# Opening of a diffusion / mLSTM layer: the first half of the tokens ahead of the second, in written order, and one weight block as a plain product

## The chip, the cores and the metric

The kernel runs on one core of a Trainium2 chip. The metric is device time in microseconds (us), the median of several runs. PE is the matrix engine (PEld its weight loads), DVE the vector engine, ACT the scalar engine, POOL the GpSimd, SP the engine that issues most transfers.

## What is computed

The reference is one layer for 128 context tokens and 512 latent tokens, d = 1024. The change touches only its first third, the first feed-forward half step with its modulated norm:

```
def adaln(cvec, w, b):
    m = jax.nn.silu(cvec) @ w + b
    return m.reshape(cvec.shape[0], N_MOD, D_MODEL)

hh = rmsnorm(x, g[0]) * (1 + m[1]) + m[0]
x = x + 0.5 * m[2] * swiglu(hh, w1, w3, w2)      # (silu(hh @ w1) * (hh @ w3)) @ w2, D_FF = 2816
hh = rmsnorm(x, g[1]) * (1 + m[4]) + m[3]
y, ctx_out = token_mixer(hh, ...)                # differential attention and mLSTM
x = x + m[5] * y
...                                              # second feed-forward half step
```

All is float32.

## The kernel before

**Layout.** The 640 tokens lie along the free axis, in two halves of 320 (`HALF`); the 1024 features are eight rows of tiles with 128 partitions (`KT`). The residual is one tile `x` of 128x8x640. Every float32 product is made of three products of a high and a low part (`mm3`: high x high, high x low, low x high): a weight tile is copied to its high part by ACT, and DVE subtracts to get the low part (`wH`/`wL`, `wB`, `wC`, `ww`); the same is done for the activations (`hm`, in `hs.hh`). The hidden width of 2816 is 11 blocks of 256 (`FB`). PE products of 128x128 by 128x320 are shown as `ps_f`.

**Opening, lines 705 to 821.** `Modulate` (705) computes the squares of all eight rows for both halves (`Stats`, 165: ACT squares, DVE adds), sums them over partitions with a product with ones (`ps_ss`), and forms 1/sqrt with a Newton step (`rstd_of`, 154) on DVE. The weights of block 0 (w1 and w3) are loaded and split in two pieces (`weights`, 719), the low parts by POOL and DVE. For each feature row k, `product` (736) multiplies the conditioning with the modulation weights `w_ada_k` (`ps_a`) and copies the result to `small`; `columns` (753) turns it into columns (`ps_at`), adds the bias and forms shift and scale for both halves, and `norm` (764) applies them. The loop of line 801 takes eight steps; each has 18 `ps_f` products: three of block 0's four units, a unit being a column half f and a token half hf, for w1 and w3. The fourth unit (1, 1) follows (814), 48 products. Then `shifts` (788) adds the shift to x itself, which `operand_sums` (330) needs.

**Blocks 1 to 10.** From block 1 on, each weight (a `Granule`, 232) is used in the seven products of a fast 2x2 scheme: over feature halves and column/token halves, `operand_sums` forms sums S1 to S4 of the activations, and `parts` and `sums` (245, 263) the sums of the weights. `parts` makes `wB` and `wC` and three `raw` steps, `sums` makes `ww` (ACT 128x2048, then DVE). One weight costs 7 x 12 = 84 products; plain it would be 96 (`Whole`, 272, does that for the down projection). `products` (406) works through the list `up_work` (509): w1 and w3 of blocks 1 to 10; of each weight the products A11, S1, S2, A12 and S3 come in turn, and the last two (A22, S4) inside the next weight's.

**Between them.** `modulation` (843) is called twice per weight; from the third weight on it lets DVE make the remaining modulation columns (`columns.tile`, 667: two reductions of 128x1024), from `raw_a` tiles that POOL's queue loads, and from `csil` (825), the conditioning, loaded by SP into a pool that takes the place of `x`.

**What sets the order.** The program is written with a tile framework: it orders the instructions of each engine by its own time estimate, and inserts the waits. Instructions passed to `keep_in_program_order` stay in the order in which they are written; before, these are all PE instructions, the table loads on ACT, and the transfers of SP's queue while `in_order` is set. Each engine works through its queue in order.

Of the kernel before, what the change touches and what calls it, by code (L numbers as in the profile page):

```python
# [31 lines left out]
def tile_trunk(ctx: ExitStack, tc: tile.TileContext, a: dict):  # L32
    nc = tc.nc
    act = nc.scalar.activation
    vec = nc.vector
    pool_e = nc.gpsimd

    def tt(eng, out, in0, in1, op):
        return eng.tensor_tensor(out=out, in0=in0, in1=in1, op=op)  # L39

    def stt(out, in0, scalar, in1, op0, op1):
        return vec.scalar_tensor_tensor(out=out, in0=in0, scalar=scalar, in1=in1, op0=op0, op1=op1)  # L42

    def ts(out, in0, s1, op0, s2=None, op1=None):
        if s2 is None:
            vec.tensor_scalar(out=out, in0=in0, scalar1=s1, scalar2=None, op0=op0)
        else:
            vec.tensor_scalar(out=out, in0=in0, scalar1=s1, scalar2=s2, op0=op0, op1=op1)
# [45 lines left out]
    for hf in range(2):  # L94
        dma(x_all[:, :, hf * HALF : (hf + 1) * HALF], a["x"][:, :, hf * HALF : (hf + 1) * HALF])
    sel = load(cp, [128, 2], a["sel"], name="sel")
    b_ada = load(cp, [128, 72], a["b_ada"], name="b_ada")
    g_norm = load(cp, [128, 3, KT], a["g_norm"], name="g_norm")
# [173 lines left out]
    class Whole(Granule):  # L272


        def split(self, fp=None):
            flat = self.raw.rearrange("p k n -> p (k n)")
            n = 512 * self.nk
            if fp is None:
# [5 lines left out]
            for (c0, c1, h), (_, _, lw) in zip(*t):  # L284
# [10 lines left out]
    class HalfStep:  # L295
# [29 lines left out]
        def gate_plain(self, f, hf, p):  # L325
            s = self.silu_tile(f, hf)
            act(s, p[0], AF.Silu)
            tt(vec, self.SO[:, self.Q[f, hf]], p[1], s, ALU.mult)

        def operand_sums(self, pair):  # L330
# [37 lines left out]
            low(S4, 0)  # L368
            low(S4, 1)
# [145 lines left out]
        def run_whole(self, x, gate, final, between):  # L515


            work = self.up_work()
# [10 lines left out]
            self.products(work, between, down[:2])  # L529
# [163 lines left out]
    with ExitStack() as ph:  # L693
# [11 lines left out]
        class Modulate:  # L705


            def __init__(self):
                self.raw, self.row = {}, {}
                self.rs = []  # L710
                x = [x_all[:, d, :] for d in range(KT)]
                st = [Stats(x, hf, ntmp) for hf in range(2)]
                for hf in range(2):
                    for d in range(KT):
                        st[hf].add(d)
                    self.rs.append(st[hf].rstd(psum))
                self.load(0)

            def weights(self, w1, w3):

                W = [[wp.tile([128, 2048], F32R, tag="w" + t, name="wH") for t in "HL"] for _ in range(2)]
                raws = [rawp.tile([128, 2048], F32, tag="raw", name="raw") for _ in range(2)]
                for k in range(2):
                    cs = slice(1024 * k, 1024 * k + 1024)
                    for raw, src, (h, lo), eng in zip(raws, (w1, w3), W, (pool_e, vec)):
                        dma(raw[:, cs], src[:, 4 * k : 4 * k + 4])
                        act(h[:, cs], raw[:, cs], AF.Copy)
                        tt(eng, lo[:, cs], raw[:, cs], h[:, cs].bitcast(F32), ALU.subtract)
                    self.load(k + 1)
                self.load(3)  # L730
                return W

            def load(self, k):
                self.raw[k] = load(fp, [128, 2048], a["w_ada_k"][k], tag=("s1", "s2", "s4", "SO")[k % 4], name="raw_a")

            def product(self, k):
# [9 lines left out]
                vec.tensor_copy(self.row[k], ps[:, :256])  # L746
                if k + 4 < KT:
                    self.load(k + 4)
                if k + 4 == KT - 1:
                    dma(ident, a["ident"])  # L750
                    in_order[0] = False

            def columns(self, k):
# [7 lines left out]
                for hf in range(2):  # L761
                    self.norm(hf, k)

            def norm(self, hf, d):

                c0 = hf * HALF
                S = hs.hh(d, hf)
                for s0, s1, j in SEGS[hf]:
                    xs = x_all[:, d, s0:s1]
                    h, lo = (t[:, s0 - c0 : s1 - c0] for t in S)  # L770
                    sh = m_of(0)[:, d, j : j + 1]
# [4 lines left out]
            def before(self, k):  # L776
                if k == 0:
                    self.product(0)
                    self.columns(0)
                    self.product(1)  # L780
                    self.columns(1)
                    self.product(2)
                elif k + 1 < KT:
                    self.columns(k + 1)
                    if k + 2 < KT:
                        self.product(k + 2)

            def shifts(self):
                for d in range(KT):
                    for s0, s1, j in ((0, NS, 0), (NS, T, 1)):  # L790
                        xs = x_all[:, d, s0:s1]
                        act(xs, xs, AF.Identity, bias=m_of(0)[:, d, j : j + 1])

        psum.order = [6, 7]
        start = Modulate()
        W = start.weights(a["w1a"][0], a["w3a"][0])
        units = [(0, 0), (1, 0), (0, 1)]
        psum.order = list(range(6))
        ps = {u: [acc_tile(psum) for _ in range(2)] for u in units}
        psum.order = [6, 7]  # L800
        for k in range(KT):
            start.before(k)
            for u in units:
                for i in range(2):
                    hs.plain(ps[u][i], W[i], *u, k)
        vec.tensor_copy(identr, ident)
        hs.begin_gated(0)
        for u in units:
            hs.gate_plain(*u, ps[u])
        for i in range(2):  # L810
            hs.up[i].load()
        psum.order = [6, 7, 0, 1, 2, 3, 4, 5]
        ps = [acc_tile(psum) for _ in range(2)]
        for i in range(2):
            for k in range(KT):
                hs.plain(ps[i], W[i], 1, 1, k)
        hs.gate_plain(1, 1, ps)
        start.shifts()
        hs.operand_sums(lambda r: x_all[:, 2 * r : 2 * r + 2, :])
        x_stack.close()  # L820
        hs.store_g(hs.SO, 0)

        ada = ExitStack()
        ada_p = ada.enter_context(tc.tile_pool(name="ada", bufs=1, side="right", reuse_waits="tile"))
        csil = ada_p.tile([128, 2, D], F32, name="csil")
        dma(csil, a["c_rows"].partition_broadcast(128))
        act(csil, csil, AF.Silu)
        nc.sync.dma_start(out=csil_dram, in_=csil[0:1])
        junk = ada_p.tile([128, D], BF16, name="junk")
# [5 lines left out]
        def load_columns(src):  # L835
            raw = ada_p.tile([128, D], F32, tag="raw", name="raw_a", bufs=2)
            nc.gpsimd.dma_start(out=raw, in_=src)
            return raw, junk

        columns.place(14, csil, load_columns)  # L840
        box = {}

        def modulation(i, at):
            if i < 20:
                if at and 2 <= i < 16:
# [56 lines left out]
        hs.run_whole(resid, half_m[:, 0], to_mixing, modulation)  # L902
# [1101 lines left out]
```

## Time and profile before

| | |
|---|---|
| median of 3 runs | 1868.25 us (1867.74 to 1875.11) |
| span of the profiled execution, first to last instruction | 1872.4 us |
| PE busy | 1812.7 us, 97% of the span |
| DVE busy | 1300.2 us, 69% |
| ACT busy | 849.6 us, 45% |
| PE in the chain of work that ended last | 86% |
| HBM read, written | 234.20 MB, 63.63 MB |

The profile is of one execution. Its span runs from the first to the last instruction; the times of the runs are measured around the whole execution, and which of them is the profiled one isn't marked. The page has the busy time of each engine, the span in 40 slices with the granted clock of PE (a share of full speed), and the costliest groups of instructions; further views of the same trace give the timeline (start, duration, engine, line, operation, output<-input, shape, count; in brackets the idle time ahead and what ended it), windows of time with the busy time of each engine, groups by shape (busy us, mean ns), and the waits.

### The profile page before, as it was taken

To read this page: it belongs to the slowest core of one execution; us is meant where nothing else is said; L and a number is where in the kernel's file an instruction comes from. 1 tells how busy PE (TensorE), PEld (TensorE's weight loads), DVE (VectorE), ACT (ScalarE), POOL (GpSimd) and SP (SyncE) were. 2 spreads that over 40 slices of the span, in tenths; PEclk is the share of its full clock that TensorE was granted. 3 is DMA by queue.
4 is the path that set the end of the run, shared out by engine and by line. 5 is a ranking of instruction groups with operands and counts; after the bars stand their busy time and mean duration, and the time that the engine had idled before them with its cause. 6 is when DMAs were issued, how large, how long until landed. Compare 5 with 4: busy or idle time off the path is not lost.

```text
span 1872.4 us, 30753 instructions
## 1 busy us (share of the span) xinstructions
PE 1812.7 (97%) x12658; PEld 1774.4 (95%) x12658; DVE 1300.2 (69%) x2177; ACT 849.6 (45%) x1455; POOL 35.8 (2%) x57
## 2 busy tenths in 40 slices
PE   5899999999999999999999989999999999999999
PEld 4899999999998999999999979999999899999999
DVE  6888886576786675865755537875456778887585
ACT  5644444112554353453454436565235645554232
POOL 1000001110000000000000000000000000000000
PEclk8899999999999999999999999999999999999999
DMA  8344547964324322322222254566442344457972
GB/s 328 119 142 168 192 169 260 382 213 146 118 81 133 123 74 95 120 77 95 98 79 83 74 178 128 187 208 218 167 134 95 130 140 153 171 177 250 336 275 91
DMA packets 127293, 299.81 MB, mean 160 GB/s; under 512 B 9457, under 2 KB 90609, under 8 KB 114353
## 3 DMA queue, kind: packets, MB, share of 16 engines
q1 hardware_dynamic: 117890, 257.49, 40.0%
q0 software_dynamic: 9264, 40.37, 5.9%
q8 instruction: 99, 1.62, 0.4%
q14 instruction: 40, 0.33, 0.0%
HBM read 234.20 MB, written 63.63 MB: 159 GB/s over the span
## 4 chain that ended last, share of the span: by engine, by line
PE 86%; DVE 7%; DMA 4%; ACT 2%; issue 1%; SPq 0%; DVEq 0%; ACTq 0%
PE ps_f L52 41%; PE ps_p L52 22%; PE ps_t L52 12%; PE ps_o L52 2%; PE sc L52 2%; PE ps_n L52 2%; PE ps_u L52 1%; DMA ada<-csil_dram 1%; PE ps_wT L55 1%; DVE ww L39 1%; PE ps_qkT L55 1%; DMA P<-nm_dram 1%; DMA so<-o_dram 0%; DVE wL L39 0%; DMA raw_a<-in_w_ada_c 0%
## 5 line engine op out<-in xcount | busy, mean ns | idle before, releaser
L52 PE MATMUL ps_f<-S,ww 128*128 128x320 f32 x1992 | 322.9, 311 | 6.7 <-ACT ww L267 4.2
L52 PEld LDWEIGHTS ps_f<-S,ww 128*128 128x128 f32 x1992 | 301.1, 189 | 9.7 <-ACT ww L267 4.5
L52 PE MATMUL ps_p<-hH,wH 128*128 128x320 f32 x864 | 274.0, 317 | 3.1 <-ACT aT L1325 2.5
L52 PE MATMUL ps_p<-hH,wL 128*128 128x320 f32 x864 | 267.3, 309 | 0.0
L52 PE MATMUL ps_p<-hL,wH 128*128 128x320 f32 x864 | 267.2, 309 | 0.0
L52 PE MATMUL ps_f<-hm,ww 128*128 128x320 f32 x1248 | 198.2, 311 | 2.0 <-DVE ww L39 2.0
L52 PEld LDWEIGHTS ps_f<-hm,ww 128*128 128x128 f32 x1248 | 188.2, 190 | 2.3 <-DVE ww L39 2.2
L52 PE MATMUL ps_t<-wH,hH 128*128 128x256 f32 x640 | 185.7, 290 | 1.0 <-DVE x L42 1.0
L52 PE MATMUL ps_t<-wH,hL 128*128 128x256 f32 x640 | 181.8, 284 | 0.0
L52 PE MATMUL ps_t<-wL,hH 128*128 128x256 f32 x640 | 181.5, 284 | 0.0
L52 PEld LDWEIGHTS ps_p<-hH,wH 128*128 128x128 f32 x864 | 162.8, 188 | 4.4 <-ACT aT L1325 2.7
L39 DVE TENSOR_TENSOR ww<-raw,ww 128x2048 fp32r<-128x2048 f32 (+1 forms) x62 | 138.7, 2237 | 37.7 <-ACT ww L267 18.7
L52 PEld LDWEIGHTS ps_p<-hL,wH 128*128 128x128 f32 x864 | 162.8, 188 | 0.5
L52 PEld LDWEIGHTS ps_p<-hH,wL 128*128 128x128 f32 x864 | 162.5, 188 | 0.0
L52 PE MATMUL ps_f<-hm,wB 128*128 128x320 f32 x1008 | 161.5, 309 | 0.0
L52 PEld LDWEIGHTS ps_f<-hm,wB 128*128 128x128 f32 x1008 | 151.3, 188 | 0.0
L39 DVE TENSOR_TENSOR wL<-raw,wH 128x2048 fp32r<-128x2048 f32 x49 | 112.1, 2289 | 38.2 <-ACT wH L123 38.1
L123 ACT ACTIVATE wH<-raw 128x2048 fp32r<-128x2048 f32 x49 | 93.6, 1911 | 89.4 <-PE ps_p L52 85.5
L39 DVE TENSOR_TENSOR raw<-raw 128x1024 f32<-128x1024 f32 x144 | 124.6, 865 | 1.9
L52 PEld LDWEIGHTS ps_t<-wH,hH 128*128 128x128 f32 x640 | 123.1, 192 | 2.0 <-issue 1.2
L52 PEld LDWEIGHTS ps_t<-wH,hL 128*128 128x128 f32 x640 | 123.1, 192 | 0.5 <-DVE hL L42 0.5
L52 PEld LDWEIGHTS ps_t<-wL,hH 128*128 128x128 f32 x640 | 123.3, 193 | 0.2
(295 smaller groups left out, 3206.0 us busy)
## 6 DMA issues: line engine op xcount, KB each, us to landing
g_dram<-g SPq DMA_DIRECT2D x44, 640.0 KB, 5.1
raw_a<-in_w_ada_c SPq DMA_DIRECT2D x24, 512.0 KB, 4.0
raw<-in_w1b SPq DMA_DIRECT2D x11, 1024.0 KB, 4.9
raw<-in_w3b SPq DMA_DIRECT2D x11, 1024.0 KB, 4.8
raw<-in_w1a SPq DMA_DIRECT2D x10, 1024.0 KB, 4.8
raw<-in_w3a SPq DMA_DIRECT2D x10, 1024.0 KB, 6.4
ada<-in_w_ada_c POOLq DMA_DIRECT2D x18, 512.0 KB, 5.3
hm<-g_dram POOLq DMA_DIRECT2D x7, 1280.0 KB, 9.6
```

What stands on the lines that cost most here:

```text
L39: return eng.tensor_tensor(out=out, in0=in0, in1=in1, op=op)
L52: tc.keep_in_program_order(nc.tensor.matmul(*args, **kw))
L55: tc.keep_in_program_order(nc.tensor.transpose(*args, **kw))
L123: act(h, raw, AF.Copy)
```

## The change

The helpers `act`, `tt`, `stt`, `ts` pass their instruction through `placed`, which keeps it in written order while `as_written` is set: through the whole opening, ACT and DVE too follow the order of the text. `Opening` takes the place of `Modulate`. x is loaded in four pieces, half 0 first; SP's queue takes modulation weights, weight pieces (four pairs instead of two) and the rest of x in turn. Squares, sums, 1/sqrt, division and norm are done for half 0 first; the first loop multiplies half 0 only (four units of w1 and w3, 12 products a step), with the squares and sums of half 1 between its steps; a second loop of eight steps then multiplies half 1. Shift and scale are applied to x at once, by ACT (half 0) or DVE (half 1). POOL makes no split any more. w1 of block 1 is split whole (into `gA`, `gB`, `CL`) and multiplied plainly, 96 products; the fast scheme begins with w3 of block 1. The last two steps of the operand sums (the lows of S4) and the start of the late columns (`csil` and its loads) move behind the first weights of the fast scheme. In the built program the PE instructions that follow block 1 are the same, in the same order; DVE and ACT differ in some places elsewhere.

```diff
+    def placed(ins):
+        if as_written[0]:
+            tc.keep_in_program_order(ins)
+        return ins
...
+    def load_x(hf, r):
+        dma(x_all[:, 4 * r : 4 * r + 4, hf * HALF : (hf + 1) * HALF], a["x"][:, 4 * r : 4 * r + 4, hf * HALF : (hf + 1) * HALF])
...
-        def operand_sums(self, pair):
+        def operand_sums(self, pair, hold=False):
...
+            def last():
+                low(S4, 0)
+                low(S4, 1)
+            if hold:
+                return last
...
-            self.products(work, between, down[:2])
+            self.products(work, between, down[:2], prepared=True)
...
-        class Modulate:
+        class Opening:
...
+            def squares(self, hf, r):
...
+                xs = x_all[:, 4 * r : 4 * r + 4, half(hf)]
+                act(p, xs[:, 0:2], AF.Square)
+                tt(vec, q, xs[:, 2:4], xs[:, 2:4], ALU.mult)
+                tt(vec, p, p, q, ALU.add)
...
+            def add_squares(self, hf, r):
+                for i in range(2):
+                    mm(self.ss[hf], ones, self.sq[r][:, i], start=r + i == 0, stop=r + i == 2)
...
+            def divide(self, hf, r):
+                xs = x_all[:, 2 * r : 2 * r + 2, half(hf)]
+                tt(vec, xs, xs, self.rs[hf][:, None, :].to_broadcast([128, 2, HALF]), ALU.mult)
...
             def norm(self, hf, d):
...
-                    stt(xs, xs, scale[:, 0, d, j : j + 1], self.rs[hf][:, s0 - c0 : s1 - c0], ALU.mult, ALU.mult)
-                    act(h, xs, AF.Identity, bias=sh)
-                    stt(lo, xs, sh, h.bitcast(F32), ALU.add, ALU.subtract)
+                    act(h[:, s0 - c0 : s1 - c0], xs, AF.Identity, scale=sc, bias=sh)
+                    if hf:
+                        ts(xs, xs, sc, ALU.mult, sh, ALU.add)
+                    else:
+                        act(xs, xs, AF.Identity, scale=sc, bias=sh)
+                tt(vec, lo, self.x[d][:, half(hf)], h.bitcast(F32), ALU.subtract)
...
+        PIECES = ((0, 2), (2, 4), (4, 6), (6, 8))
+        def step(ps, k, hf, between=None):
+            h, lo = hs.hh(k, hf)
+            for m, (w, v) in enumerate(((0, h), (1, h), (0, lo))):
+                for (f, i), p in ps.items():
+                    col = 256 * k + 128 * f
+                    mm(p, W[i][w][:, col : col + 128], v, start=k == 0 and m == 0, stop=k == KT - 1 and m == 2)
+                if m == 0 and between is not None:
+                    between()
...
+        for r in range(2):
+            start.squares(0, r)
+            start.add_squares(0, r)
+        start.product(0)
+        start.load(4)
+        load_weights(3)
+        start.rstd(0)
+        split_weights(0, "high")
+        start.refine(0)
+        start.columns(0)
+        start.divide(0, 0)
+        start.product(1)
+        split_weights(0, "low")
+        start.norm(0, 0)
+        start.load(5)
...
+        first = acc()
...
         for k in range(KT):
+            def ahead(k=k):
+                if k + 1 < KT:
+                    start.columns(k + 1)
+                if k == 5:
+                    start.refine(1)
+                if k >= 6:
+                    start.divide(1, k - 6)
+                if k % 2 and k < 6:
+                    split_weights((k + 1) // 2, "low")
+                elif k % 2 == 0 and k + 2 < KT:
+                    start.divide(0, (k + 2) // 2)
+                if k + 1 < KT:
+                    start.norm(0, k + 1)
+                if k % 2 == 0 and k < 6:
+                    split_weights(k // 2 + 1, "high")
+            step(first, k, 0, ahead)
+            if k + 2 < KT:
+                start.product(k + 2)
+                if k < 2:
+                    start.load(k + 6)
+            if k in (3, 4):
+                start.add_squares(1, k - 3)
+            if k in (1, 2):
+                start.squares(1, k - 1)
+            if k == 4:
+                start.rstd(1)
+            if k >= 6:
+                start.norm(1, k - 6)
...
+        for k in range(KT):
+            if k + 2 < KT:
+                if k in (1, 3):
+                    start.divide(1, (k + 3) // 2)
+                start.norm(1, k + 2)
+            step(second, k, 1)
+            if k == 5:
+                whole.split(t=[((0, 2048, w1[0]),), ((0, 1792, w1[1]), (1792, 2048, w1[2][:, :256]))])
...
+        for f, hf in ((0, 1), (1, 1), (0, 0), (1, 0)):
+            p = acc_tile(psum)
+            for k in range(KT):
+                mm3(p, whole.w(0, k, f), whole.w(1, k, f), *hs.hh(k, hf), k == 0, k == KT - 1)
+            gate_first(f, hf, p, None)
+        with tc.issue_after(end.ins), tc.issue_after(at_act.ins):
+            last_lows = hs.operand_sums(lambda r: x_all[:, 2 * r : 2 * r + 2, :], True)
...
+        def begin_columns():
+            with tc.issue_after(hs.work[1][0].split_at):
+                last_lows()
+            x_stack.close()
...
+                if (i, at) == (1, 1):
+                    begin_columns()
...
-        hs.run_whole(resid, half_m[:, 0], to_mixing, modulation)
+        hs.run_whole(resid, half_m[:, 0], to_mixing, lambda i, at: modulation(i + 1, at))
```

More of the change, by code (lines that the diff above doesn't have):

```diff
@@ L272, in tile_trunk, with split @@
     class Whole(Granule):
-        def split(self, fp=None):
+        def split(self, fp=None, t=None):
             flat = self.raw.rearrange("p k n -> p (k n)")
             n = 512 * self.nk
-            if fp is None:
+            if t is not None:
+                pass
+            elif fp is None:
                 t = [((0, n, h),) for h in self.two(wp, "w", 2048, None)]
@@ L703, in tile_trunk @@
         hs = HalfStep(1, fp, ntmp, psum, a["w1a"], a["w3a"], a["w2a"], FB)
-        class Modulate:
+        class Opening:
             def __init__(self):
[L709 to L731, printed above, removed]
@@ L745, in product @@
                 self.row[k] = mrow[k % 2]
[L746 to L751, printed above, removed]
+                placed(vec.tensor_copy(self.row[k], ps[:, :256]))
             def columns(self, k):
@@ L776, in before @@
[L776 to L800, printed above, removed]
-        for k in range(KT):
[L802 to L806, printed above, removed]
@@ L807, in tile_trunk @@
-        hs.begin_gated(0)
[L808 to L814, printed above, removed]
-            for k in range(KT):
[L816 to L820, printed above, removed]
@@ L821, in tile_trunk @@
-        hs.store_g(hs.SO, 0)
[L823 to L829, printed above, removed]
+                    xs, sc, sh = self.x[d][:, s0:s1], scale[:, 0, d, j : j + 1], m_of(0)[:, d, j : j + 1]
@@ new lines, in tile_trunk, with load_weights, split_weights @@
+        PIECES = ((0, 2), (2, 4), (4, 6), (6, 8))
+        def load_weights(i):
+            k0, k1 = PIECES[i]
+            for raw, src in zip(raws, (a["w1a"][0], a["w3a"][0])):
+                dma(raw[:, 256 * k0 : 256 * k1], src[:, k0:k1])
+        def split_weights(i, part):
+            cs = slice(256 * PIECES[i][0], 256 * PIECES[i][1])
+            for raw, (h, lo) in zip(raws, W):
+                if part != "low":
+                    act(h[:, cs], raw[:, cs], AF.Copy)
+                if part != "high":
+                    tt(vec, lo[:, cs], raw[:, cs], h[:, cs].bitcast(F32), ALU.subtract)
@@ new lines, in step @@
+        def step(ps, k, hf, between=None):
[6 more added lines that the diff above has]
+                    between()
+        acc = lambda: {(f, i): acc_tile(psum) for f in range(2) for i in range(2)}
@@ new lines, in tile_trunk @@
+        as_written[0] = True
+        start = Opening()
+        start.load(0)
+        for t, n in ((sel, "sel"), (b_ada, "b_ada"), (g_norm, "g_norm")):
+            dma(t, a[n])
+        load_weights(0)
+        start.load(1)
+        start.load(2)
+        load_x(1, 0)
+        load_weights(1)
+        start.load(3)
+        load_x(1, 1)
+        load_weights(2)
+        psum.order = [4, 5, 6]
+        for r in range(2):
+            start.squares(0, r)
+            start.add_squares(0, r)
+        start.product(0)
@@ new lines, in tile_trunk @@
+        dma(ident, a["ident"])
+        in_order[0] = False
+        hs.work = hs.up_work()
+        _, _, gate_first, _ = hs.work.pop(0)
+        whole = Whole(4, hs.up[0].fetch)
+        whole.load()
+        hs.up[1].load()
+        hs.begin_gated(0)
+        psum.order = [4, 5, 6, 7, 0, 1, 2, 3]
+        second = acc()
+        w1 = [fp.tile([128, n], F32R, tag=tag, name="w" + tag, bufs=bufs) for tag, n, bufs in (("gA", 2048, 1), ("gB", 1792, 1), ("CL", 512, 3))]
+        for k in range(KT):
[6 more added lines that the diff above has]
+                whole.split(t=[((0, 2048, w1[0]),), ((0, 1792, w1[1]), (1792, 2048, w1[2][:, :256]))])
+                hs.up[2].load()
+                silu_table()
+                for f in range(2):
+                    hs.gate_plain(f, 0, (first[f, 0], first[f, 1]))
@@ L830, in tile_trunk @@
+        with tc.issue_after(end.ins), tc.issue_after(at_act.ins):
+            hs.work[0][0].parts(fp)
+            hs.work[0][0].sums()
+        hs.store_g(hs.SO, 0)
         columns = Columns(56)
@@ L835, in load_columns @@
         def load_columns(src):
-            raw = ada_p.tile([128, D], F32, tag="raw", name="raw_a", bufs=2)
+            raw = ada_p[0].tile([128, D], F32, tag="raw", name="raw_a", bufs=2)
             nc.gpsimd.dma_start(out=raw, in_=src)
-            return raw, junk
-        columns.place(14, csil, load_columns)
+            return raw, ada_p[1]
+        ada = ExitStack()
+        ada_p = []
+        def begin_columns():
+            with tc.issue_after(hs.work[1][0].split_at):
+                last_lows()
+            x_stack.close()
+            pool = ada.enter_context(tc.tile_pool(name="ada", bufs=1, side="right", reuse_waits="tile"))
+            csil = pool.tile([128, 2, D], F32, name="csil")
+            dma(csil, a["c_rows"].partition_broadcast(128))
+            act(csil, csil, AF.Silu)
+            nc.sync.dma_start(out=csil_dram, in_=csil[0:1])
+            ada_p.extend((pool, pool.tile([128, D], BF16, name="junk")))
+            columns.place(14, csil, load_columns)
         box = {}
```

71 lines of the change are left out of this document (49 added, 22 removed).

## The prediction

> **What bounds the kernel now.** First the page, for where the matrix engine is not busy:
>
> ```profile
> span 1872.4 us, 30753 instructions
> ...
> PE   5899999999999999999999989999999999999999
> ...
> PEclk8899999999999999999999999999999999999999
> ```
>
> One slice is 46.8 us. PE is full from the third slice on; the first two miss some 50% and over 10%, at a reduced clock. The stages in windows (us, PE, PEld, DVE, ACT and POOL busy, granted clock, DMA share, GB/s) say how much is at stake:
>
> ```profile
> 0.00:100.00 100.00, 75.18 (x507) 65.11 (x508) 75.76 (x141) 59.34 (x103) 6.37 (x8) 0.90 0.57 216
> 100.00:380.00 280.00, 277.25 (x1869) 275.40 (x1868) 217.54 (x289) 116.01 (x157) 16.71 (x28) 0.99 0.63 219
> ```
>
> 25 us of the first 100 are idle, 2.75 of the next 280. The timeline of the opening (start, duration) shows which:
>
> ```profile
> 8.01 0.47 ACT L177 ACTIVATE nacc<-x 128x320 f32<-128x320 f32 x1 [4.07 <-DMA x<-in_x]
> ...
> 12.41 1.44 PE L52 MATMUL ps_ss<-nacc,ones 128*128 128x320 f32 x2 [12.41 <-DVE nacc L39]
> ...
> 14.95 0.49 DVE L48 TENSOR_SCALAR rv<-ps_ss 128x320 f32<-128x320 f32 x1
> ...
> 17.73 2.35 POOL L39 TENSOR_TENSOR wH<-raw,wH 128x1024 fp32r<-128x1024 f32 x1 [17.28 <-ACT wH L727]
> 17.78 2.65 DVE L42 SCALAR_TENSOR_TENSOR ry<-rt,ry 128x320 f32<-128x320 f32 x1
> ...
> 22.89 1.07 PE L52 MATMUL ps_a<-raw_a,small 128*32 128x256 f32 x16
> ...
> 30.23 4.83 PE L52 MATMUL ps_f<-hm,wH 128*128 128x320 f32 x18
> ...
> 36.33 2.90 PE L52 MATMUL ps_f<-hm,wH 128*128 128x320 f32 x18
> ...
> 40.51 2.90 PE L52 MATMUL ps_f<-hm,wH 128*128 128x320 f32 x18
> ...
> 84.27 0.90 PE L52 MATMUL ps_f<-S,ww 128*128 128x320 f32 x2 [4.22 <-ACT ww L267]
> ...
> 86.60 3.04 PE L52 MATMUL ps_f<-S,ww 128*128 128x320 f32 x10 [1.42 <-DVE ww L39]
> ...
> 96.11 1.92 PE L52 MATMUL ps_f<-hm,wB 128*128 128x320 f32 x12
> ...
> 108.44 1.92 PE L52 MATMUL ps_f<-hm,wB 128*128 128x320 f32 x12
> ```
>
> Two losses: no product of block 0 starts before 30.23, and PE waits 4.22 + 1.42 us for the split weight sums ww of block 1. From 96.11 (block 2's first weight) to 108.44 (its second) 84 products take 12.33: 0.147 us each, no gap. **Both kernels run the same PE stream from there to the end, so the sum is kept at these two marks.** Each loss has a tail at half clock (us, PE busy, granted clock, DMA share, GB/s):
>
> ```profile
> 22.00:24.00 2.00, 1.61 (x20) 1.00 1.02 422
> 24.00:26.00 2.00, 0.00 (x0) 0.57 1.03 426
> ...
> 34.00:36.00 2.00, 2.00 (x22) 0.87 1.02 422
> ...
> 80.00:82.00 2.00, 0.06 (x1) 1.00 0.94 326
> 82.00:84.00 2.00, 0.00 (x0) 0.58 0.80 194
> ...
> 92.00:94.00 2.00, 2.00 (x14) 0.86 0.03 8
> ```
>
> 0.57 means full clock for 0.28 us of the two, so it fell at 24.3 and rose at 34.5; again at 82.3 and 92.6: both times 10.2 us.
>
> **The change part by part.**
>
> *Start of block 0.* The bytes of the first half still land at 8.0. Its squares become one ACT and two DVE instructions on 128x640 per two pairs of rows; the last pair costs two DVE operations of 0.82 (row x<-x below): 9.7 instead of 12.41. From 12.41 to 14.95 two products with ones take 2.5; so 12.3. Next on PE stands the modulation product 0 (1.07 at full clock), and on DVE its copy (0.42) now stands ahead of rv: 13.8. Then rv 0.49, two ACT steps 0.9, three DVE steps of 0.49, mod and scale 0.3, the division 0.82, the ACT norm 0.65: 18.9. **I take 19.0 against 30.23.** The 2.65 for ry, five times rv's 0.49, began with a POOL split (17.73); that split goes, its work moves to DVE as pieces of 128x512.
>
> ```profile
> 490.42 0.70 PE L52 MATMUL ps_ss<-nacc,ones 128*128 128x320 f32 x2
> ...
> L39 DVE TENSOR_TENSOR x<-x 128x640 f32<-128x640 f32 x8 | 6.4, 818 | 0.0
> ...
> L42 DVE SCALAR_TENSOR_TENSOR x<-x,scale,ry 128x192 f32<-128x192 f32 x8 | 3.3, 411 | 0.0
> ...
> L1838 ACT ACTIVATE hm<-x,mod,scale 128x320 fp32r<-128x320 f32 x8 | 4.5, 648 | 0.0
> ...
> L1838 ACT ACTIVATE hm<-x,mod,scale 128x192 fp32r<-128x192 f32 x8 | 4.3, 535 | 2.5 <-DVE x L39 2.5
> ...
> L354 ACT ACTIVATE S<-x 128x640 fp32r<-128x640 f32 x6 | 4.3, 732 | 0.8 <-issue 0.5 <-DVE x L39 0.3
> ...
> L39 DVE TENSOR_TENSOR ww<-raw,ww 128x2048 fp32r<-128x2048 f32 x6 | 13.7, 2291 | 7.0 <-PE ps_f L52 3.7 <-ACT ww L267 3.3
> ...
> L267 ACT ACTIVATE ww<-raw 128x2048 fp32r<-128x2048 f32 x6 | 11.5, 1912 | 8.5 <-PE ps_f L52 8.4
> ...
> L39 DVE TENSOR_TENSOR wB<-raw,wB 128x1024 fp32r<-128x1024 f32 x6 | 7.3, 1222 | 0.7 <-ACT wB L252 0.7
> ...
> L39 DVE TENSOR_TENSOR wC<-raw,wC 128x512 fp32r<-128x512 f32 x7 | 4.8, 685 | 0.0
> ...
> L39 DVE TENSOR_TENSOR g<-SO,g 128x1280 fp32r<-128x1280 f32 x3 | 4.5, 1485 | 0.0
> ...
> L676 DVE CUSTOM_DVE_ANT_0 junk<-raw_a,csil 128x1024 bf16<-128x1024 f32 x6 | 7.3, 1218 | 0.0
> ```
>
> *First half, eight steps.* Before, 36.33 to 40.51 is 4.18 for 18 products: 2.64, plus 1.54 for the modulation. A step now has 12 products: 1.76 + 1.54 = 3.3, six times; the last two have less modulation (2.3 and 1.8): 23.9. The second half's sums now stand inside: two pairs at about 1.1 (from 490.42, at full clock): 2.2. Half clock for the first step or so: +2 (18 products took 4.83, not 2.9). Written order on DVE: two squares (1.5) stand ahead of mod and scale of row 3; ACT's two norm steps (1.3) and the low (0.5) come after, then the copy that step 3's ps_at needs: PE, with 2.2 of products and 1.0 of modulation to do meanwhile, waits some 0.7. In step 5 the refinement (1.5), two splits (1.4), a low (0.5) and the copy (0.4), 3.7 after the scale, stand ahead of step 6's ps_at; PE has 2.3: 1.4. Sum 30.2, **end at 49.2**. Loads: 13.1 MB of x, modulation and first weights at the 0.42 MB/us of the windows, 1.31 of them landed by 8.0, end near 37; SP's queue is now x, modulation and weight pieces in turn, and its last modulation weight is needed at about 43. Block 1's two weights stand behind it and behind the last split (45), land some 8 later and are needed at 59. Hidden.
>
> *Second half and the plain product.* 96 products each: 14.1 + 14.1, **77.4**. The second half's norm runs ahead under them: per row of tiles ACT 0.54 + under 0.5, DVE at most 0.41 + 0.35 (two pieces, priced as the two-tensor form), a low of 0.49 and half a division, 1.7, against PE's 1.76. Nothing is charged; without that cover, 0.3 a step. The plain form has 96 products where 84 stood: 12 x 0.147 = 1.8, in the sum.
>
> *Block 1's second weight.* Its S1 needs ww. ACT in its queue waits for the silu of the plain product's third unit (end 73.9) before the copy of S2's second half: silu 0.43, copy 0.73, then DVE: three lows and two terms at about 0.74 (818 ns less overlap), ww 2.29: 81.1. PE has done its first product at 79.2: **a wait of 1.9** takes the place of 4.22 + 1.42 and their tail. Four more products: block 2's mark at 88.1 against 96.11, **8.0 ahead**.
>
> *Given back after it.* Next ww: wB 1.14, wC 0.6, g 1.4, raw 1.14 + 0.6 + 0.6, the ACT half 1.91, ww 2.29 = 9.7 after the last ww; PE takes five products, 8.8: **0.9**. The late columns: the load of csil now stands behind the S4 lows, 1.9 after that ww. From there 5.1 to ACT (below), 1.91 of silu, 2.6 for two reductions that stand ahead of the next ww, 2.29: 11.9, while PE has 12.3 - 1.9 = 10.4: **1.5**.
>
> ```profile
> 81.30 0.35 SPq L74 DMA_DIRECT2D csil<-in_c_rows  x1
> ...
> 86.41 1.91 ACT L827 ACTIVATE csil<-csil 128x2048 f32<-128x2048 f32 x1 [2.19 <-DMA csil<-in_c_rows]
> ```
>
> **Sum: 8.0 - 0.9 - 1.5 = 5.6 us gained.** The rest of the program keeps its PE order; some DVE and ACT instructions change places under a full PE: 0, at most 1 either way. The profiled span of 1872.4 becomes 1866.8. That span is 4.15 above the median of 1868.25 (runs from 1867.74 to 1875.11; what lies around the span comes on top and stays), so the gain is taken off the median: **1862.6**.
>
> *Unknown costs.* The half clock in the first step: between 0 (already at full clock) and twice 2. The two waits in the loop: 0 to 4. The three ww waits: 0 each if ACT and DVE run as they do after 96, or up to before's 5.6 for the first; I take the queues as added up, since every instruction in them has a row. Bounds together: 5.6 + 4.3 + 2.1 + 1 = 13 gained, 5.6 - 2 - 1.9 - 3.7 = 2 lost, and 1 for the order elsewhere: 1855 to 1871.
>
> *A rule weighed.* The clock fell at 24.3 although PE had been busy 1.61 of the two us before 24; at 82.3 it fell 2.4 us after PE's last work near 79.9. So something between a stretch with gaps and 2.4 us of idle suffices, and 1.9 us of waiting may. [...]
>
> **The rivals.**
>
> 1. *The waits don't come* (DVE and ACT get ahead): the three ww waits (4.3) and the loop's 2.1 go, gain 11 to 12: 1857. For it: ACT is at 59% in the opening. Against: the queues hold an order that PE's progress gates (silu ahead of copies).
> 2. *The start is early but given back*: the loop runs at DVE's pace. DVE has some 23 us of work in the 30 (copies, splits, divisions, lows and squares at the durations above), in written order, each step waiting for ps_at; 0.7 us more per step for semaphores takes 5.6: 1868. That is also where it ends if the early start is only spent waiting. For it: before, DVE is 76% busy here and the chain of waits runs through it.
> 3. *Half clock again, slower*: the place is the S1 wait, and again the csil wait. If the first grows to before's 4.2 (+2.3), the clock falls and ten microseconds pass at half of it (+5); the same at csil: 14.6 against a gain of 5.6: 9 slower, about 1877. It decides below the 2.4 us of idle after which the clock fell at 82.3, at 1.9 to 2.4. For it: just this happened at 82.3. Against: my waits are 1.9 and less, with a full PE before and after.
>
> **How the numbers follow.** Forecast (gain 3 to 9.3) 0.48; rival 1 0.27; rival 2 (gain under 3, loss under 3) 0.18; rival 3 0.07. Faster or slower by 0.5% is 9.3 us, about what a measurement of this kernel can tell from no change: faster 0.27, same 0.67, slower 0.06. The range takes in the forecast, most of rivals 1 and 2: 1855 to 1871.
>
> **What would show it.** Right: first ps_f product near 19; the last of the first half near 49; the plain product's last near 77; one wait of some 2 us for ww after it; block 2's marks near 88 and 101. Wrong: a loop of 35 us or more, granted clock at 0.5 after 26 or after 80, or a first block 2 mark after 93; on the other side, no wait for ww at all.

## The result, and the profile after

The change made the kernel a little slower. Over 20 runs of each, the changed kernel took 1875.92 us (median, 1870.05 to 1882.19) and the kernel before 1873.76 (1867.74 to 1876.32); the ratio is 1.0018, 95% interval 1.001 to 1.0025. The forecast was 1862.6, 5.6 below a median of three runs, 1868.25; with more runs that median itself stands 5.5 higher.

The page of the changed kernel: span, busy tenths of PE in 40 slices, and granted clock.

```profile
span 1874.8 us, 30757 instructions
...
PE   7999999999999999999999989999999899999999
...
PEclk9999999999999999999999999999999899999999
```

The first slices, which the change is about, are fuller (7 and 9 where 5 and 8 stood). But the slice near 1500 us, which was full before, now shows an 8 in both rows (the slice from 1453 to 1500). The windows (us, PE busy, granted clock, DMA share, GB/s) of after put sizes to it:

```profile
0.00:100.00 100.00, 82.62 (x575) 0.97 0.58 215
100.00:380.00 280.00, 276.74 (x1874) 1.00 0.65 227
380.00:1480.00 1100.00, 1070.55 (x7618) 0.99 0.37 124
1480.00:1510.00 30.00, 25.86 (x159) 0.89 0.52 177
```

and the last of these windows in the kernel before:

```profile
1480.00:1510.00 30.00, 30.00 (x205) 1.00 0.63 229
```

PE gained 7.4 busy us in the first 100, and lost 4.1 in thirty microseconds that lie 1400 us further on, in code that the change doesn't touch: the opening of the second feed-forward half step. The timeline of PE after (start, duration, engine, line, operation, tiles, shape, count, idle time ahead and its releaser), first in the opening:

```profile
18.64 1.08 PE L59 MATMUL ps_f<-hm,wH 128*128 128x320 f32 x4 [2.43 <-ACT hm L43]
...
63.29 0.46 PE L59 MATMUL ps_f<-hm,wgA 128*128 128x320 f32 x2
...
77.37 1.92 PE L59 MATMUL ps_f<-hm,wB 128*128 128x320 f32 x12
79.13 0.46 PE L59 MATMUL ps_f<-S,ww 128*128 128x320 f32 x2
81.23 3.49 PE L59 MATMUL ps_f<-S,ww 128*128 128x320 f32 x22 [1.64 <-DVE ww L46]
84.56 1.92 PE L59 MATMUL ps_f<-hm,wB 128*128 128x320 f32 x12
89.22 2.31 PE L59 MATMUL ps_f<-S,ww 128*128 128x320 f32 x12 [2.75 <-ACT u L43]
91.33 3.22 PE L59 MATMUL ps_f<-hm,wB 128*128 128x320 f32 x12
94.38 1.92 PE L59 MATMUL ps_f<-S,ww 128*128 128x320 f32 x12
```

Up to 85 this is the forecast to 0.4 us: first product at 18.64 (19.0 forecast), plain product from 63.29 to 77.37 (77.4), a wait of 1.64 for ww (1.9). Then comes a wait that the forecast hasn't: 2.75 us for the copy u, and a stretch at half clock behind it (granted 0.50 from 91 to 94; 3.22 us for twelve products that take 1.92 elsewhere). In the second half step the two kernels' PE rows, after:

```profile
1485.15 1.92 PE L59 MATMUL ps_f<-hm,wB 128*128 128x320 f32 x12
1489.46 0.57 PE L59 MATMUL ps_f<-S,ww 128*128 128x320 f32 x2 [2.38 <-ACT ww L43]
1491.79 3.04 PE L59 MATMUL ps_f<-S,ww 128*128 128x320 f32 x10 [1.76 <-DVE ww L46]
1494.62 3.03 PE L59 MATMUL ps_f<-hm,ww 128*128 128x320 f32 x12
1497.48 1.92 PE L59 MATMUL ps_f<-S,ww 128*128 128x320 f32 x12
```

and before:

```profile
1490.00 1.92 PE L52 MATMUL ps_f<-hm,wB 128*128 128x320 f32 x12
1491.76 2.17 PE L52 MATMUL ps_f<-S,ww 128*128 128x320 f32 x12
1493.77 1.92 PE L52 MATMUL ps_f<-hm,ww 128*128 128x320 f32 x12
1495.53 1.92 PE L52 MATMUL ps_f<-S,ww 128*128 128x320 f32 x12
```

Where PE was 4.85 us ahead (1485.15 against 1490.00) it leaves 1.95 late (1497.48 against 1495.53): 6.8 us lost on 36 products, 4.1 by waiting and the rest at half clock (granted 0.50 from 1492 to 1496, where before had 1.00).

Following the same product in both traces gives where the lead stood:

| product | before | after | lead |
|---|---|---|---|
| block 2's first weight, A11 | 99.64 | 91.33 | 8.3 |
| the S1 products behind it | 101.39 | 94.38 | 7.0 |
| first product of the token mixer (ps_t) | 488.19 | 480.37 | 7.8 |
| second half step, second weight, A11 | 1490.00 | 1485.15 | 4.9 |
| 36 products later | 1495.53 | 1497.48 | -1.95 |
| last row of PE | 1866.93 | 1869.15 | -2.2 |

Of the 7.8 at the token mixer, 1.5 is not the change's work. The kernel before lost it near 360, where its clock fell behind a wait of 1.96 (0.70 from 358 to 360, then 0.50; last section): the same product stands at 357.91 and 351.61 ahead of that, 6.3 apart, and at 362.76 and 354.94 behind it, 7.8 apart.

### The profile page after: what moved, and what is told of

Its sections match the earlier page's. It is cut to its first block, busy times and chain, and to the rows that moved or that the text cites. A ratio compares the mean times of both kernels' runs of the same rounds, so it can differ in the third digit from the quotient of the medians.

```text
span 1874.8 us, 30757 instructions
## 1 busy us (share of the span) xinstructions
PE 1816.8 (97%) x12678; PEld 1776.7 (95%) x12678; DVE 1295.3 (69%) x2165; ACT 842.7 (45%) x1435; POOL 31.0 (2%) x55
## 4 chain that ended last, share of the span: by engine, by line
PE 83%; DVE 8%; DMA 5%; ACT 2%; issue 1%; SPq 0%; DVEq 0%; ACTq 0%
PE ps_f L59 39%; PE ps_p L59 20%; PE ps_t L59 12%; PE ps_o L59 2%; PE sc L59 2%; PE ps_n L59 2%; DMA ada<-csil_dram 1%; DVE ww L46 1%; PE ps_wT L62 1%; PE ps_qkT L62 1%; DMA P<-nm_dram 1%; PE ps_u L59 1%; DMA hm<-g_dram 1%; DVE raw_a L697 1%; PE ps_ss L59 1%
## 5 line engine op out<-in xcount | busy, mean ns | idle before, releaser
L59 PE MATMUL ps_f<-S,ww 128*128 128x320 f32 x1956 | 315.9, 311 | 9.5 <-DVE ww L46 4.0
L59 PEld LDWEIGHTS ps_f<-S,ww 128*128 128x128 f32 x1956 | 294.4, 188 | 12.4 <-DVE ww L46 6.7
L43 ACT ACTIVATE ww<-raw 128x2048 fp32r<-128x2048 f32 (+1 forms) x61 | 114.1, 1871 | 157.6 <-PE ps_f L59 97.1
L43 ACT ACTIVATE wH<-raw 128x2048 fp32r<-128x2048 f32 (+1 forms) x57 | 98.2, 1729 | 89.0 <-PE ps_p L59 84.3
```

What stands on the lines that cost most here:

```text
L43: return placed(nc.scalar.activation(*args, **kw))
L59: tc.keep_in_program_order(nc.tensor.matmul(*args, **kw))
```

## The experiments

Two theories stood against each other at either place. **Order:** the instruction that PE waits for is ready to run, but stands behind others in the queue of ACT or DVE, which wait themselves. **Rival:** its data comes when it comes (a load, a chain that doesn't move with PE), so that any lead is eaten there. The queues' orders can be edited without touching anything else: the listing of the built program gives the order on each engine, and edges that order issue only, with no wait for completion, pin it.

```diff
+    def queue(engine, order):
+        ins = [i for i in tc.nc.cur_bb.bb.instructions if str(i.engine) == engine and ...]
+        for p, n in zip(order, order[1:]):
+            tc.add_manual_dep(ins[-n], ins[-p].name, mybir.DependencyInfo(mybir.DependencyClass.NoSync, ...), reason="queue")
```

In all of these but fast_w1 every other instruction on PE, ACT, DVE and POOL keeps its place; with the order of the second half step, two loads of x on SP move too. The first two runs exchange that place between the kernels.

**late_as_before.** The changed kernel with 19 ACT and 27 DVE instructions near 1470 to 1500 in the order of before. The core of it on ACT:

```diff
 u
-wB
-s
-u
-s
-ps_f
+wC
 ww
+wB
+s
+u
+ps_f
+s
```

> The changed kernel, whose ACT and DVE queues stand in the order of the kernel before in one place only: the opening of the second feed-forward half step, near 1470 to 1500 us (19 ACT and 27 DVE instructions). Theory T (the lead is lost there to the order of the two queues): the waits of 2.38 and 1.76 for ww at 1487 to 1492 and the half clock behind them go, 6.8 us less than the changed kernel, 1869 against the 1873.8 of the kernel before, ratio near 0.9975. Rival R (ww comes at 1492 in both kernels because something that does not move with the lead delivers it, so the order is not the cause): the waits stay, 1876, ratio near 1.002.

Measured: 1871.19 (11 runs), ratio to before 0.9993 (0.9984 to 1.0001); the changed kernel stood at 1.0018. The wait for ww is gone, as PE's rows of this run show:

```profile
1486.67 1.92 PE L59 MATMUL ps_f<-hm,wB 128*128 128x320 f32 x12
1488.43 1.92 PE L59 MATMUL ps_f<-S,ww 128*128 128x320 f32 x12
```

ww is there at 1488.4, so nothing holds it until 1492: the rival falls. In the traces the place is worth what was expected: this execution came to it 1.5 us behind that of the changed kernel (A11 of the half step's first fast weight at 1477.87 against 1476.35) and left it 5.5 ahead (1491.95 against 1497.48 for the product behind the 36), 7 us in all. By the medians and by the two ratios the gain is 4.7 us, less than 6.8; where the other runs lose the rest is not shown.

**before_late_as_after.** The same edit the other way round: the kernel before, with the changed kernel's order in that place.

> The kernel before, with the ACT and DVE orders of the changed kernel in the same one place, the opening of the second feed-forward half step. Theory T: the waits of some 4 us and half clock of up to 2.6 us behind them appear, 4 to 7 us more, 1878 to 1881, ratio 1.002 to 1.0037. Rival R: nothing changes, ratio 1.000.

Measured: 1878.52 (6 runs), ratio 1.0040 (1.0028 to 1.0051), 6.3 us more than before's median beside it (1872.25). The two waits appear with the same lengths, to 0.01 us:

```profile
1490.84 0.56 PE L52 MATMUL ps_f<-S,ww 128*128 128x320 f32 x2 [2.38 <-ACT ww L267]
1493.17 3.04 PE L52 MATMUL ps_f<-S,ww 128*128 128x320 f32 x10 [1.77 <-DVE ww L39]
```

So the order alone, without any of the change's own edits, costs what the changed kernel lost there. Why it is slow is on ACT and DVE, in the changed kernel:

```profile
1484.41 0.42 ACT L43 ACTIVATE s<-ps_f 128x320 f32<-128x320 f32 x1
1485.35 0.44 ACT L43 ACTIVATE u<-ps_f 128x320 f32<-128x320 f32 x1 [0.52 <-PE ps_f L59]
1486.35 0.47 ACT L43 ACTIVATE s<-s 128x320 f32<-128x320 f32 x1 [0.56 <-DVE s L46]
1487.17 0.42 ACT L43 ACTIVATE ps_f<-ps_f 128x320 f32<-128x320 f32 x1 [0.35 <-PE ps_f L59]
1487.51 1.90 ACT L43 ACTIVATE ww<-raw 128x2048 fp32r<-128x2048 f32 x1
```

and on DVE:

```profile
1485.82 0.49 DVE L46 TENSOR_TENSOR s<-ps_f,u 128x320 f32<-128x320 f32 x1 [1.39 <-ACT u L43]
1486.23 0.68 DVE L46 TENSOR_TENSOR raw<-raw 128x512 f32<-128x512 f32 x1
```

The ACT half of ww, which PE needs for its next product, stands behind four small instructions, of which the last can only run when PE has ended the product just before the wait (A11, 1485.15 to 1487). So the splitting of ww starts when PE is already idle, and takes 1.90 on ACT and 2.29 on DVE. ACT alone is not the whole of it: ww also needs the last raw step, and DVE made that only at 1486.23 to 1486.91, behind a step s that waited 1.39 for a copy u, which itself waits for PE. By these rows a better order on ACT alone could have started ww at most 0.6 us earlier. In late_as_before, where both queues stand in the order of before, DVE has the raw steps done by 1483.31 and ACT starts ww at 1484.20, 2.5 us ahead of A11. The two queues were only exchanged together; the share of each was not measured.

**u_first.** In the opening of the changed kernel, ACT's queue after the S4 copies was:

```profile
79.67 1.35 ACT L43 ACTIVATE hm<-x 128x640 fp32r<-128x640 f32 x2
86.15 0.63 ACT L43 ACTIVATE wC<-raw 128x512 fp32r<-128x512 f32 x1 [5.13 <-DMA raw<-in_w3a]
86.94 1.91 ACT L43 ACTIVATE ww<-raw 128x2048 fp32r<-128x2048 f32 x1 [0.16 <-DVE raw L46]
88.75 0.42 ACT L43 ACTIVATE u<-ps_f 128x320 f32<-128x320 f32 x1
```

wC belongs to block 2's second weight, whose load was issued at 81.20, when ww of block 1 had freed its buffer (its DVE half ended at 81.17). The copy u, which PE needs for its next product, could have run when S2 ended, at 84.7; it waits until 88.75 behind a load that is needed a whole weight later. In this trace ACT took nothing out of turn: it stood idle for the 5.13 us ahead of wC, and u ran third, behind wC and ww, as the queue has them. The edit:

```diff
 hm hm
+u
 wC
 ww
-u
 wB
```

> The changed kernel with all queues as built but one ACT instruction: the copy u of block 1's second weight stands two places further ahead, before the copy wC of block 2's second weight (which waits 5.13 us for its load) and before ww. Theory: PE's wait of 2.75 at 86.5 to 89.2 goes and so does the half clock of about 1.7 behind it; S1 of block 2's first weight then waits about 1.3 for ww, and some 0.8 comes back at the late columns: 2.5 to 3.3 less than the changed kernel, about 1873, ratio near 1.0000. Rival (the copy only waits for PE's own S2, which ends at 83, or PE then waits as long for ww): less than 1 us less, ratio 1.0015. The place near 1490 is as in the changed kernel by both.

Measured: 1877.92 (7 runs), ratio 1.0033 (1.0021 to 1.0044): no gain. PE's rows of this run:

```profile
86.91 1.92 PE L59 MATMUL ps_f<-hm,wB 128*128 128x320 f32 x12
88.67 1.92 PE L59 MATMUL ps_f<-S,ww 128*128 128x320 f32 x12
...
93.58 1.73 PE L59 MATMUL ps_f<-S,ww 128*128 128x320 f32 x10 [0.94 <-DVE ww L46]
...
108.08 2.37 PE L59 MATMUL ps_f<-S,ww 128*128 128x320 f32 x10 [1.91 <-DVE ww L46]
110.24 2.86 PE L59 MATMUL ps_f<-hm,ww 128*128 128x320 f32 x12
```

The wait for u is gone, as expected; but the next two waits are now 0.94 and 1.91, and behind the second the clock fell, by the rows' lengths (2.37 and 2.86 for rows of 1.73 and 1.92), which cost some 1.6 us more. The 2.75 had been covering the two that the prediction had summed as 0.9 and 1.5. The account comes out at nothing: 2.75 and the half clock of 1.7 behind it went, 0.94, 1.91 and 1.6 came. This execution also ran at half clock until 27.0 at its start and so stood 2.4 us behind the changed kernel's before the edit (A11 of block 1's second weight at 79.73 against 77.37); it is 2.3 behind after these waits (S2 of that next weight at 112.94 against 110.65). That the edit brings nothing by itself is what times and rows both say; that u's wait came from the order is what the rows say.

**both_orders.** u_first and late_as_before together.

> The changed kernel with both edits: the copy u two places further ahead, and the opening of the second feed-forward half step in the order of the kernel before. Theory T: 9 to 10 us less than the changed kernel, about 1866.5, ratio near 0.996. If the losses are not of these orders: 1873 to 1876, ratio 1.000 to 1.002.

Measured: 1869.99 (12 runs), ratio 0.9988 (0.9979 to 0.9997). It beats the kernel before, but by a third of what was expected: the waits of 1.64, 0.94 and 2.00 still stand in the opening.

**queues_by_need.** both_orders, with the ACT and DVE queues of block 1 in the order in which PE needs them: ww ahead of the last S3 low and of the S4 terms, raw steps ahead of g, u ahead of the S4 copies, the third ww ahead of csil's silu and of the column reductions. On DVE, from 75 us:

```diff
 S S
-S x x
 ww
+S
 wB wC
-g
 raw raw raw
+x x
 ww
```

> The kernel of both_orders with the ACT and DVE queues of block 1 put in the order in which PE needs them: ww of block 1's second weight ahead of the S3 low and the S4 terms, the raw steps of the next weight ahead of the S4 terms and of g, the copy u and ww ahead of the S4 copies, and the third ww with its three raw steps ahead of csil's silu and the two column reductions. Theory T (each wait of PE after 78 us stands in these queues, not in a transfer): the waits of 1.64, 0.94 and 2.00 of both_orders go to 0.5 or less each, block 2's first weight begins near 87 and its second near 99, 4 us less than both_orders: about 1866, ratio 0.9965. Rival (the raw loads set the pace, so the waits move to wC or to the next ww): 1870, ratio 0.9988, with a wait for ww of 1 us or more still in the opening.

Measured: 1871.49 (11 runs), ratio 1.0003 (0.9993 to 1.0012). All three waits are gone or small (0.27 at most for ww), as the theory had it; the time is not, since one of 6.86 for the next u has come: on ACT, csil's silu, now ahead of it, waited 6.15 for its load, issued at 93.33 behind two others and landed at 105.7.

**csil_first.** One SP instruction moved, csil's load ahead of those two.

```diff
+csil
 g_dram
 raw
-csil
```

> The kernel of queues_by_need with one SP instruction moved: the load of csil goes out ahead of the second g transfer and of the raw load of block 3's first weight, instead of behind them. Theory (the 6.86 us wait of queues_by_need is the csil load, issued at 93.3 behind these two and landed at 105.7, with csil's silu ahead of the copy u on ACT): csil lands near 97 to 100, the wait for u goes, and what remains is both_orders without its waits of 1.64, 0.94 and 2.00: 3 to 4 us less than both_orders, about 1866.5, ratio 0.9965 to 0.9975. Rival (the wait is not the load's place in the queue but its bytes, 8 loads and stores sharing the same engines): the wait stays at 3 us or more, 1869 to 1871, ratio near 0.999.

Measured: 1869.59 (12 runs), ratio 0.9986 (0.9974 to 0.9997). csil's silu now ran at 101.00 without a wait; but behind it on ACT stood wC of block 3's first weight, waiting for its load until 106.54, and behind that again u: PE waited 4.36. That load, now behind csil and g, had taken from 94.27 to 106.5. By its numbers the rival holds: with this order of ACT, the load that went last was the one waited for in both runs (6.15 us for csil in queues_by_need, 3.64 for this one here).

**copies_first.** So the copies of that weight go behind u, on ACT and DVE:

```diff
 ww csil
-wC
 g
-wB
 s u ps_f
+wC wB
 s s u
```

> The kernel of csil_first with the copies of block 3's first weight (wC, wB on ACT, then on DVE) behind the copy u of block 2's first weight instead of ahead of it: in csil_first wC waited until 106.5 for its load and u stood two places behind, so PE waited 4.36 and the clock fell. Theory (the head of ACT's queue waits for a load that is needed later): that wait goes, no wait for u or ww of 0.5 us or more is left between 78 and 125, and the time is 4 to 6 us less than csil_first's profile, 3 less than both_orders: about 1866.5, ratio 0.9965. Rival (each wait that is taken away comes up at the next weight, since the raw loads land at their own pace): a wait for ww or wB of 2 us or more in the next weight, 1869 to 1871, ratio near 0.9985.

Measured: 1865.31 (7 runs) beside 1872.88 of before (12 runs): ratio 0.9962 (0.9947 to 0.9976), 7.6 us faster than before, and the fastest of all versions. PE's rows:

```profile
79.28 3.72 PE L59 MATMUL ps_f<-S,ww 128*128 128x320 f32 x24
...
86.35 1.92 PE L59 MATMUL ps_f<-hm,wB 128*128 128x320 f32 x12
88.11 0.46 PE L59 MATMUL ps_f<-S,ww 128*128 128x320 f32 x2
88.84 1.73 PE L59 MATMUL ps_f<-S,ww 128*128 128x320 f32 x10 [0.28 <-DVE ww L46]
...
104.05 2.02 PE L59 MATMUL ps_f<-hm,ww 128*128 128x320 f32 x12 [0.54 <-ACT u L43]
```

Block 2's first weight begins at 86.35, 13.3 us ahead of before's 99.64; the waits left are 0.28 to 0.54. Against the changed kernel no product was left out, and in the opening only csil's load was moved among the transfers: the rest of what it gains on that kernel came from what stood ahead of what on ACT and DVE. Not all of the 13.3 reaches the end: 11.4 are left at 104.05 (before: 115.47), and 8.1 at PE's last row (1858.80 against 1866.93). Part of that is the clock, 0.83 from 530 to 540 and from 560 to 570 in this execution, where before's was 1.00 from 530 to 590.

**fast_w1.** The changed kernel without its plain product: block 1's first weight in the fast scheme again.

```diff
-        _, _, gate_first, _ = hs.work.pop(0)
-        whole = Whole(4, hs.up[0].fetch)
-        whole.load()
+        hs.up[0].load()
         hs.up[1].load()
...
-        for f, hf in ((0, 1), (1, 1), (0, 0), (1, 0)):
-            p = acc_tile(psum)
-            for k in range(KT):
-                mm3(p, whole.w(0, k, f), whole.w(1, k, f), *hs.hh(k, hf), k == 0, k == KT - 1)
-            gate_first(f, hf, p, None)
```

> The changed kernel without its plain product: block 1's first weight is multiplied in the fast scheme again (84 products for 96), all else as changed. Theory: the plain product covers the operand sums; without it S1 of that weight stands at 65 and waits until its ww and the S1 sums are made, between 72 and 79, and some of the time behind it goes at half clock; the waits of 1.64 for ww and 2.75 for u of the changed kernel go. Block 2's first weight begins at 95 to 103 (91.3 in the changed kernel), the time is 4 to 11 us over the changed kernel, ratio 1.004 to 1.008. Rival (the plain product costs its 1.8 us and covers nothing): 1.8 us less, ratio 1.0008. The opening of the second half step may be ordered anew by the build, which can add or take up to 7 us; the mark of block 2 is free of that.

Measured: 1887.26 (4 runs), ratio 1.0085 (1.0071 to 1.0099); block 2's first weight at 103.89, 12.6 later than in the changed kernel, a little over the range. But 2.5 of the 12.6 stand there before the plain product's place (65.82 against 63.29 for the first product behind the two loops): half clock in the first loop lasted until 27.2 in this execution and until 22.5 in the changed kernel's. The edit itself is worth some 10.

```profile
65.82 1.92 PE L59 MATMUL ps_f<-hm,wB 128*128 128x320 f32 x12
78.20 0.90 PE L59 MATMUL ps_f<-S,ww 128*128 128x320 f32 x2 [10.46 <-ACT ww L43]
82.14 4.88 PE L59 MATMUL ps_f<-S,ww 128*128 128x320 f32 x22 [3.04 <-DVE ww L46]
```

Without the plain product's 14.1 us PE waits 13.5 for ww, whose split stands behind the operand sums in ACT's queue, and pays half clock on top (4.88 us for 22 products that take 3.49 in the changed kernel). With the queues as these two builds order them, the plain product earns its 12 extra products many times over; whether another order of ACT and DVE would have done without it was not tried.

## Why the prediction was wrong

1. **Start, first loop, second half, plain product, S1 wait:** right, to 0.4 us in every mark. In the start a sum slipped: from 13.8 on, the terms given add up to 18.4, not 18.9; the measured 18.64 lies between. The terms of 0.9 and 1.5 did not show in the changed kernel (0 and 0.15), where the wait for u came first; with that wait gone they came at 0.94 and 1.91 in u_first, 0.94 and 2.00 in both_orders. Adding up the queues row by row works where the order of the queue is known.
2. **"Block 2's mark at 88.1 against 96.11":** two different products. 88.1 was worked out for A11 of block 2's first weight; the row at 96.11 is A12 of the weight before it (the rows behind it run S3, then A11 at 99.64). Counted right, the forecast's own numbers made 11.5 us ahead, not 8.0. The tile names alone don't tell A11 from A12 (both read wB); the neighbours do: A11 and S1 are followed by hm,ww of the weight before.
3. **"Four more products":** failed. S3 waited 2.75 for u, and half clock behind it took 0.4 and 1.3; so the lead was 7.0 and not 11.5. The prediction walked ACT's queue for ww, but not for u; the order wC, ww, u was to be seen in the built program, and its own sum had the first ww done at 81.1, which is when wC's load could go out (81.20 in the trace).
4. **"Some DVE and ACT instructions change places under a full PE: 0, at most 1 either way":** failed, and it is the step that turned the sign: 6.8 us lost on 36 products, where 1 was the bound. The listing showed the moves in the second half step's opening; there PE is full only because ww comes in time (before, a row of 2.17 where others take 1.92). Both exchanges of that order price it: 4.7 us taken away, 6.3 added.
5. **The rivals.** The third had the mechanism (half clock behind a longer wait), but at another instruction, S3, and with 1.7 us of half clock where 5 were priced: the clock rose again after some 3.5 us and not after ten (granted 0.89 from 90 to 91, 0.50 to 94, 0.91 from 94 to 95). That its 1877 lies 1 us from the measured 1875.92 is luck: the bulk was lost near 1490, where it had nothing. The second, start given back, describes the outcome, but not at its place: DVE's pace in the loop held.
6. **The baseline.** 1868.25 was the median of three runs; 20 runs give 1873.76.

Between the mixer's start and 1440 the lead went from 7.8 to 4.9. Of this 1.5 is one fall of the clock (next section but one); the rest is small differences in many waits, and was not tested. Whether the opening as built, without the loss near 1490, is faster than before isn't settled either: late_as_before's interval reaches from 0.9984 to 1.0001.

## What to carry to other kernels

When a scheduler orders the queues by its own estimates, a change at one end can reorder code at the other that nobody touched; list the built order of every engine, and at each place that moved ask which instruction PE needs next and what now stands ahead of it. Here u stood behind a head that waited for a load needed later (5.13 us for wC, 6.15 for csil's silu in queues_by_need), and ww behind small instructions that waited for PE's own progress (started at 1487.51, and at 1484.20 in late_as_before); put copies that PE needs at once ahead of copies for the next weight. And removing one wait showed the next (2.75 and 1.7 of half clock went in u_first; 0.94, 1.91 and 1.6 came): price the chain of them, not the one on top.

## What was not expected of the hardware

The clock didn't answer a given wait in a given way here. In the mixer PE waits 1.72 us for the copy kpk in both kernels; after (us, PE busy, granted clock, DMA share, GB/s) the clock fell behind it,

```profile
532.00:534.00 2.00, 0.99 (x11) 1.00 0.00 0
534.00:536.00 2.00, 2.00 (x13) 0.63 0.03 8
536.00:538.00 2.00, 2.00 (x12) 0.52 0.00 0
```

and before it did not:

```profile
538.00:540.00 2.00, 1.11 (x10) 1.00 0.00 0
540.00:542.00 2.00, 1.17 (x12) 1.00 0.00 0
542.00:544.00 2.00, 2.00 (x19) 1.00 0.03 8
```

That fall cost 1.5 us. The kernel before and before_late_as_after are the same program up to 1470; in the one a wait of 1.96 at 356 brought the clock down (0.70, then 0.50), in the other one of 1.99 at 354 did not. Across it the second's lead over the first went from 1.9 us (356.00 against 357.91) to 3.4 (359.33 against 362.76). The half clock at the start of block 0 likewise ended anywhere from 22.5 (the changed kernel) to 27.2 (fast_w1). Single runs of one kernel differ by up to 12 us here; these falls are likely a good part of it (of the changed kernel's 20 runs the fastest, 1870.05, had a mean granted clock of 0.992, the slowest, 1882.19, one of 0.986), so a change of a few microseconds needs its trace beside its time. What decides whether a wait brings the clock down was not shown: waits of 1.72 and 1.96 us did in these executions, and waits of 1.72 and 1.99 did not.

The load of csil took longer where more was issued close ahead of it and beside it: 5.9 us from its issue to its silu in u_first (95.42 to 101.37), 1.9 us behind a raw load, and 12.4 in queues_by_need (93.33 to 105.75), 0.5 us behind a raw load, 1.0 behind a g transfer and with two loads raw_a that POOL's queue had issued from 91.19 on (in u_first from 96.04, behind csil). Which of these made the difference was not tested.
